# Token mixer: one lead product for v, a and b, and one logarithm and one exponential for all lengths

## The chip, the cores and the metric

The kernel runs on one core of one Trainium2 chip. The metric is the device time of one execution in microseconds (us), the median of several runs.

## What is computed

Two layers, each of a feed-forward (swiglu), a token mixer, a second feed-forward and a gated projection, each ended by a layer norm; behind them a second block with attention and a mixture of experts, which the change does not touch. There are S = 256 tokens of D = 1024. The token mixer is this (the reference, cut):

```python
proj = h @ w_in                    # sb q,k,v 3 x 256 | gdn q,k,v 3 x 512 | z 512 | a 4 | b 4 | sc 3 x 256
o_sb = stick_breaking_attention(sb_q, sb_k, sb_v)
gdn_qkv = silu(causal_dwconv(gdn_qkv, gdn_conv_w))
g_q = l2_normalize(g_q) * (GDN_HEAD_DIM ** -0.5)      # t * rsqrt(sum(t*t) + eps), over a head's 128
g_k = l2_normalize(g_k)
beta = sigmoid(gdn_b)
log_decay = -exp(gdn_a_log) * softplus(gdn_a + gdn_dt_bias)
o_gdn = gated_rms_norm(gated_delta_rule_chunked(g_q, g_k, g_v, log_decay, beta), gdn_z, gdn_norm_w)
o_sc = sc_b * causal_dwconv(sc_c * sc_h, sc_conv_w)
return concatenate([o_sb, o_gdn, o_sc]) @ w_out
```

## The kernel before, in words

Tokens lie in two halves of 128 (`t` is 0 or 1). Every large product is made three times in a reduced type, high by high, high by low and low by high part (`mm3`, L318 to L320, and the same three in `proj_T`, L559). The input of a stage is transposed on PE (`transpose_split`, L339) and split into `xTh` and `xTl`. Weights come by SP's DMAs (L254) into three raw buffers of 1 MB (`wraw`); ACT copies the high part (`whi`, L323) and DVE subtracts for the low part (`wlo`, L324), tile by tile of 512 columns. `proj` makes tokens by columns (tile `pj`); `proj_T` makes columns by tokens (tile `pT`, 256 wide, both halves at once).

Each stage's first weights are led: they are loaded and split in the tail of the stage before, four of the eight blocks of 128 rows by `start_next` (tiles `ghi`, `glo`) and the rest by `start_rest`. For the mixer these are z's 512 columns.

The mixer's order in the code (`token_mix`) is: z (`gdn_z`, led, 48 products of 512 columns); a and b (`gdn_ab`: a load of eight columns of its own, 24 products with eight output rows into `g_abT`, L588, a copy, two small transposes `g_abp`, L593, a copy); k and q of the delta rule with their convolution (`gdn_part`, L681 and L683); the gates; silu; the lengths (`gdn_norm` and `l2n`); stick-breaking's q and k; the delta rule's v; then stick-breaking's v (`usev`, 48 products of 256 columns); then the delta rule's preparation (L743 to L830) and a weave of its scan (L855 to L891) with stick-breaking's steps (tile `sb`); the short convolution (tile `sc`); the output projection.

`l2n` runs four times, for two groups of heads of k and of q: ACT squares (L692), one product with a 128 x 128 matrix of ones sums over the partitions and spreads the sum to all of them (tile `l2p`, L694, one PSUM bank at a time), ACT takes Ln and then Exp (L109, tile `l2sq`), DVE multiplies (L697). Behind each, DVE multiplies the row factors (`g_br` for k, L714; `g_eg` for q, L718). The products of k with itself (`pkk`, L755) need them.

Within an engine the order is set by a scheduler from the code's order, from priorities (`later`, `behind`) and from a model of due times; it weaves independent work between dependent steps. A matrix product in the full type (the lengths, the transposes, the delta rule's small products) and one in the reduced type alternate on PE.

Of the kernel before, what the change touches and what calls it, by code (L numbers as in the profile page):

```python
# [8 lines left out]
F32 = mybir.dt.float32  # L9
F32R = mybir.dt.float32r  # L10
I32 = mybir.dt.int32
AF = mybir.ActivationFunctionType
ALU = mybir.AluOpType
AX = mybir.AxisListType
PSUM = bass.MemoryType.PSUM
P = 128
CH = (slice(0, 64), slice(64, 128))

S = 256
D = 1024  # L20
NT = S // P
KD = D // P
# [6 lines left out]
OFF_SB = 0  # L29
OFF_GDN = 768  # L30
OFF_Z = 2304
OFF_AB = 2816
# [20 lines left out]
class Net:  # L53
# [107 lines left out]
    def masks(self):  # L161
        nc = self.nc
        g = nc.gpsimd
# [55 lines left out]
        for i in range(2):  # L219
            m = self.c([P, P], f"csel{i}")  # L220
# [5 lines left out]
        self.c_lns = self.c([P, 1], "c_lns")  # L226
        g.memset(self.c_lns, math.log(128 ** -0.5))

# [19 lines left out]
    def piece(self, src, kk, n, by=0):  # L248

        nc = self.nc  # L250
        m = kk * n
        raw = self.raw()
        rv = raw[:, :m].rearrange("p (k n) -> p k n", k=kk)
        nc.sync.dma_start(out=rv, in_=src.rearrange("(k p) n -> p k n", p=P))  # L254
        k2, n2 = (min(kk, 1024 // n), n) if by == 0 else (kk, min(n, 1024 // kk))
# [49 lines left out]
    def start_rest(self):  # L305
        if self.leads:
            src, other = self.leads.pop(0)
            if other is not None:
                self.led_p = self.piece_k(other, 2, D)
            self.led += self.piece_k(src[512:], 4, src.shape[1])  # L310
# [268 lines left out]

    def gdn_ab(self, i):  # L580

        nc, a = self.nc, self.a
        xT = self.xT
        (hi, lo), = self.piece(a["mix_w_in"][i][:, OFF_AB:OFF_AB + 8], KD, 8)
        o = self.mm_bank("g_abT")
        for k in range(KD):
            for n, (w, z) in enumerate(((hi, xT[0]), (lo, xT[0]), (hi, xT[1]))):
                nc.tensor.matmul(o[:8, :S], w[:, k], z[:, k], start=k == 0 and n == 0, stop=k == KD - 1 and n == 2)  # L588
        abT = self.s("g_abTs")
        nc.vector.tensor_copy(abT[:8, :S], o[:8, :S])  # L590
        pt = self.tr_bank("g_abp")
        for t in range(NT):
            nc.tensor.transpose(pt[:, t * 8:t * 8 + 8], abT[:8, t * P:t * P + P], self.ident[:8, :8])  # L593
        ab = self.tmp.tile([P, 8, 2], F32, name="g_ab", bufs=2)
        nc.vector.tensor_copy(ab, pt[:, :16].rearrange("p (t n) -> p n t", t=2))
        return ab

    def gdn_gates(self, i, ab):
# [88 lines left out]

    def l2n(self, src, out, bias):

        nc = self.nc  # L690
        sq = self.s("l2sq")
        nc.scalar.activation(sq, src, AF.Square)  # L692
        pn = self.tr_bank("l2p")
        nc.tensor.matmul(pn, self.ones, sq, start=True, stop=True)  # L694
        self.tact(sq, pn, AF.Ln, bias=self.c_eps)
        self.tact(sq, sq, AF.Exp, scale=-0.5, bias=bias)
        nc.vector.tensor_tensor(out, src, sq, ALU.mult)  # L697

# [9 lines left out]
    def gdn_norm(self, G, k, q):  # L708

        v = self.nc.vector  # L710
        for gr in range(2):
            eg, br = G["rows"][gr]
            self.l2n(k[gr], k[gr], 0.0)
            v.tensor_tensor(br, k[gr], br, ALU.mult)  # L714
        for gr in range(2):
            eg, br = G["rows"][gr]
            self.l2n(q[gr], q[gr], self.c_lns)
            v.tensor_tensor(eg, q[gr], eg, ALU.mult)  # L718
# [87 lines left out]

    def gdn_z(self, i):
        nc, a = self.nc, self.a
        nw = self.tmp.tile([P, P], F32, name="gdn_nw", bufs=2)
        nc.sync.dma_start(out=nw, in_=a["gdn_norm_w"][i:i + 1].broadcast_to([P, P]))  # L810
        zs = {}

        def use(t, o):
            z = zs[t] = self.s("zs")
            self.tact(z, o, AF.Silu)
            z4 = z.rearrange("p (n w) -> p n w", n=4)
            self.after(nc.vector.tensor_tensor(z4, z4, self.bc(nw, 4), ALU.mult).ins, self.ln_end)

        self.proj(a["mix_w_in"][i][:, OFF_Z:OFF_Z + 512], 512, use, lead=True)
        return zs  # L820

# [90 lines left out]

    def stick_breaking(self, i, mT):

        nc, a = self.nc, self.a
        mm = nc.tensor.matmul
        w = a["mix_w_in"][i]
        q, k, v = self.s("sbq"), self.s("sbk"), self.s("sbv")
        for dst, c0 in ((q, 0), (k, 256)):
# [4 lines left out]
        yield self.gdn_part(i, 8)  # L924

        def usev(t, o):
            nc.scalar.activation(v[:, t * 256:t * 256 + 256], o, AF.Copy)
        self.proj(w[:, 512:768], 256, usev, bank=lambda t, name: self.mm_bank(name))
        yield

# [75 lines left out]
    def token_mix(self, i):  # L1006
        a = self.a
        mT = self.new_xT()
        zs = self.gdn_z(i)
        ab = self.gdn_ab(i)  # L1010
        k, q = self.gdn_part(i, 4), self.gdn_part(i, 0)
# [7 lines left out]
        self.gdn_norm(G, k, q)  # L1019
        heads = self.stick_breaking(i, mT)  # L1020
        vc = next(heads)
# [3 lines left out]
        self.act_set(LOG_SET)  # L1025
        next(heads)
        with self.later(-1500):
# [956 lines left out]
    def run(self, stages=("f", "m", "f2", "p", "2")):  # L1984
# [4 lines left out]
        of = dict(f=lambda i: (a["ffn_w_in"][i, 0][:, :512], None),  # L1989
                  m=lambda i: (a["mix_w_in"][i][:, OFF_Z:OFF_Z + 512], None),  # L1990
                  f2=lambda i: (a["ffn_w_in"][i, 1][:, :512], None),
# [61 lines left out]
```

## Time and profile before

| | us |
|---|---|
| median of 3 runs | 1670.34 |
| lowest and highest run | 1666.17 and 1672.14 |
| profiled execution, its own time | 1672.71 |
| its span | 1670.9 |
| PE busy in the span | 1614.5 |
| DVE busy | 1289.5 |
| ACT busy | 899.0 |

The profile is of one execution. Its rows give the start or the sum and the duration in us; "x" counts instructions; `out<-in` are the program's tile names; a bracket tells how long the engine stood idle before the row and what released it. PE's records of neighbouring products overlap, so what a product occupies is the distance from one start to the next. A product in the full type leaves two records.

### The profile page before, as it was taken

To read this page: it belongs to the slowest core of one execution; us is meant where nothing else is said; L and a number is where in the kernel's file an instruction comes from. 1 tells how busy PE (TensorE), PEld (TensorE's weight loads), DVE (VectorE), ACT (ScalarE), POOL (GpSimd) and SP (SyncE) were. 2 spreads that over 40 slices of the span, in tenths; PEclk is the share of its full clock that TensorE was granted. 3 is DMA by queue.
4 is the path that set the end of the run, shared out by engine and by line. 5 is a ranking of instruction groups with operands and counts; after the bars stand their busy time and mean duration, and the time that the engine had idled before them with its cause. 6 is when DMAs were issued, how large, how long until landed. Compare 5 with 4: busy or idle time off the path is not lost.

```text
span 1670.9 us, 24511 instructions
## 1 busy us (share of the span) xinstructions
PE 1614.5 (97%) x9247; PEld 1346.8 (81%) x9247; DVE 1289.5 (77%) x2389; ACT 899.0 (54%) x1593; POOL 24.4 (1%) x90
## 2 busy tenths in 40 slices
PE   8999999999999999999999999999889889999998
PEld 6888888888888878888888888888677678787876
DVE  7669886677679786688876686697978569899896
ACT  6543374554543445543555554544575367677674
POOL 2000000000000000000000000000200000000000
PEclk9999999999999999999999999999899789999999
DMA  8667562236568656665532365685344129899995
GB/s 298 201 210 259 190 186 73 87 133 227 181 235 285 205 162 210 202 247 201 177 102 102 133 200 178 205 304 203 126 151 134 47 101 363 314 339 323 367 339 195
DMA packets 175197, 342.45 MB, mean 205 GB/s; under 512 B 12970, under 2 KB 49891, under 8 KB 175075
## 3 DMA queue, kind: packets, MB, share of 16 engines
q1 hardware_dynamic: 175074, 340.84, 59.6%
q8 instruction: 74, 1.21, 0.3%
q14 instruction: 49, 0.39, 0.1%
HBM read 339.76 MB, written 1.05 MB: 204 GB/s over the span
## 4 chain that ended last, share of the span: by engine, by line
PE 86%; DVE 7%; ACT 3%; DMA 2%; issue 1%; SPq 0%; DVEq 0%; ACTq 0%
PE gu L318 10%; PE gu L319 9%; PE gu L320 9%; PE pT L559 5%; PE y L320 5%; PE y L318 5%; PE y L319 5%; PE moe_h L319 3%; PE moe_h L320 3%; PE moe_h L318 3%; PE sc L559 2%; PE moe_y L319 2%; PE moe_y L318 2%; PE moe_y L320 2%; PE pt L339 2%; PE pj L318 2%
## 5 line engine op out<-in xcount | busy, mean ns | idle before, releaser
L324 DVE TENSOR_TENSOR wlo<-wraw,whi 128x512 fp32r<-128x512 f32 (+3 forms) x752 | 605.8, 837 | 165.2 <-ACT whi L323 162.2
L323 ACT ACTIVATE whi<-wraw 128x512 fp32r<-128x512 f32 (+3 forms) x752 | 528.4, 746 | 355.9 <-issue 98.5
L318 PE MATMUL gu<-whi,xTh 128*128 128x512 f32 (+1 forms) x736 | 274.8, 373 | 0.0
L319 PE MATMUL gu<-wlo,xTh 128*128 128x512 f32 (+1 forms) x736 | 274.2, 373 | 0.0
L320 PE MATMUL gu<-whi,xTl 128*128 128x512 f32 (+1 forms) x736 | 273.7, 372 | 0.0
L318 PEld LDWEIGHTS gu<-whi,xTh 128*128 128x128 f32 x736 | 138.7, 188 | 23.3
L320 PEld LDWEIGHTS gu<-whi,xTl 128*128 128x128 f32 x736 | 138.7, 188 | 23.2
L319 PEld LDWEIGHTS gu<-wlo,xTh 128*128 128x128 f32 x736 | 138.8, 189 | 22.7
L318 PE MATMUL y<-whi,hTh 128*128 128x512 f32 x224 | 87.7, 391 | 0.0
L320 PE MATMUL y<-whi,hTl 128*128 128x512 f32 x224 | 87.6, 391 | 0.0
L319 PE MATMUL y<-wlo,hTh 128*128 128x512 f32 x224 | 87.2, 389 | 0.0
L318 PE MATMUL y<-whi,xTh 128*128 128x512 f32 x192 | 75.9, 395 | 0.0
L320 PE MATMUL y<-whi,xTl 128*128 128x512 f32 x192 | 75.2, 392 | 0.0
L319 PE MATMUL y<-wlo,xTh 128*128 128x512 f32 x192 | 74.8, 390 | 0.0
L559 PE MATMUL pT<-xTh,whi 128*128 128x256 f32 x256 | 74.6, 291 | 0.0
L559 PE MATMUL pT<-xTh,wlo 128*128 128x256 f32 x256 | 74.4, 291 | 0.0
L559 PE MATMUL pT<-xTl,whi 128*128 128x256 f32 x256 | 73.4, 288 | 0.0
L1167 DVE SCALAR_TENSOR_TENSOR ada<-ada_w,silu_c,ada 128x512 f32<-128x512 f32 x84 | 62.7, 747 | 9.1 <-DMA ada_w<-in_w_ada_dram 8.4
L1280 DVE SCALAR_TENSOR_TENSOR bias<-rel_m,rel_delta,bias 128x384 f32<-128x384 bf16 x116 | 63.9, 613 | 0.5
L109 ACT ACTIVATE ffn_h<-gu 128x512 f32<-128x512 f32 (+1 forms) x48 | 27.0, 563 | 56.3 <-PE gu L320 56.3
L323 ACT ACTIVATE xTh<-pt 128x512 fp32r<-128x512 f32 (+1 forms) x72 | 35.6, 500 | 39.7 <-PE pt L339 34.2
L319 PE MATMUL moe_h<-wlo,moe_xh 128*128 128x512 f32 x128 | 50.8, 397 | 1.7 <-DVE wlo L324 1.7
(573 smaller groups left out, 3276.8 us busy)
## 6 DMA issues: line engine op xcount, KB each, us to landing
wraw<-in_ffn_w_in_dram SPq DMA_DIRECT2D x88, 1024.0 KB
wraw<-in_ffn_w_out_dram SPq DMA_DIRECT2D x44, 1024.0 KB
wraw<-in_mix_w_in_dram SPq DMA_DIRECT2D x28, 1024.0 KB
ada_w<-in_w_ada_dram SPq DMA_DIRECT2D x96, 256.0 KB
wraw<-in_w_gate_dram SPq DMA_DIRECT2D x20, 1024.0 KB
wraw<-in_w_up_dram SPq DMA_DIRECT2D x19, 1024.0 KB
wraw<-in_w_down_dram SPq DMA_DIRECT2D x19, 1024.0 KB
wraw<-in_mix_w_out_dram SPq DMA_DIRECT2D x8, 1024.0 KB
```

The costliest lines, as they stand in the source:

```text
L109: ins = self.nc.scalar.activation(*args, **kw).ins
L318: mm(out, l[0], r[0], start=start, stop=False)
L319: mm(out, l[0], r[1], start=False, stop=False)
L320: mm(out, l[1], r[0], start=False, stop=stop)
L323: h = self.split_hi = self.nc.scalar.activation(hi, src, AF.Copy).ins
L324: self.mark = self.nc.vector.tensor_tensor(lo, src, hi.bitcast(F32), ALU.subtract).ins
L339: self.nc.tensor.transpose(pt[:, j * P:(j + 1) * P], src[:, (c + j) * P:(c + j + 1) * P], self.ident)
L559: self.nc.tensor.matmul(o[:, :S], w[:, k], z[:, k], start=k == 0 and n == 0, stop=k == KD - 1 and n == 2)
L1167: z = nc.vector.scalar_tensor_tensor(acc, raw, c, acc, ALU.mult, ALU.add)
L1280: z = nc.vector.scalar_tensor_tensor(b, m, d, b, ALU.mult, ALU.add)
```

## The change

z and stick-breaking's v become one step at the stage's start (`mix_in`). Its second set of weights holds v's 256 columns and the eight of a and b side by side, 264 wide, and is led like z's (`led_p`, two pieces of 512 rows, four DMAs). For each half of the tokens it makes z's product and then the 264-wide one; ACT copies v, DVE copies a and b straight from PSUM. `gdn_ab` and `usev` go. `l2n` now runs once for all four: four squares, four sums with 32 columns of ones, each into its own quarter of 32 rows of one PSUM bank; one Ln and one Exp over the bank, with the bias of k on the lower 64 rows and of q on the upper 64; four products of one row each with a row of ones (tile `l2b`) spread the four results over 128 rows, and DVE multiplies from PSUM.

```diff
--- before.py
+++ after.py
@@ -224,7 +224,9 @@
         self.c_eps = self.c([P, 1], "c_eps")
         g.memset(self.c_eps, NORM_EPS)
         self.c_lns = self.c([P, 1], "c_lns")
-        g.memset(self.c_lns, math.log(128 ** -0.5))
+
+        g.memset(self.c_lns[0:64], 0.0)
+        g.memset(self.c_lns[64:P], math.log(128 ** -0.5))
 
     def bc(self, m, n):
 
@@ -251,7 +253,11 @@
         m = kk * n
         raw = self.raw()
         rv = raw[:, :m].rearrange("p (k n) -> p k n", k=kk)
-        nc.sync.dma_start(out=rv, in_=src.rearrange("(k p) n -> p k n", p=P))
+        n0 = 0
+        for z in src if isinstance(src, tuple) else (src,):
+            n1 = n0 + z.shape[1]
+            nc.sync.dma_start(out=rv[:, :, n0:n1], in_=z.rearrange("(k p) n -> p k n", p=P))
+            n0 = n1
         k2, n2 = (min(kk, 1024 // n), n) if by == 0 else (kk, min(n, 1024 // kk))
         k2 = -(-kk // -(-kk // k2))
         out = []
@@ -305,7 +311,9 @@
     def start_rest(self):
         if self.leads:
             src, other = self.leads.pop(0)
-            if other is not None:
+            if isinstance(other, tuple):
+                self.led_p = [z for k in (0, 512) for z in self.piece_k(tuple(w[k:k + 512] for w in other), 4, 264)]
+            elif other is not None:
                 self.led_p = self.piece_k(other, 2, D)
             self.led += self.piece_k(src[512:], 4, src.shape[1])
 
@@ -576,24 +584,6 @@
                 for k in range(k0, k1):
                     self.mm3(acc[t][:, :n], lhs(k, tt), pc[k - k0], k == 0, k == K - 1)
         return [use(t, acc[t][:, :n]) for t in range(NT)]
-
-    def gdn_ab(self, i):
-
-        nc, a = self.nc, self.a
-        xT = self.xT
-        (hi, lo), = self.piece(a["mix_w_in"][i][:, OFF_AB:OFF_AB + 8], KD, 8)
-        o = self.mm_bank("g_abT")
-        for k in range(KD):
-            for n, (w, z) in enumerate(((hi, xT[0]), (lo, xT[0]), (hi, xT[1]))):
-                nc.tensor.matmul(o[:8, :S], w[:, k], z[:, k], start=k == 0 and n == 0, stop=k == KD - 1 and n == 2)
-        abT = self.s("g_abTs")
-        nc.vector.tensor_copy(abT[:8, :S], o[:8, :S])
-        pt = self.tr_bank("g_abp")
-        for t in range(NT):
-            nc.tensor.transpose(pt[:, t * 8:t * 8 + 8], abT[:8, t * P:t * P + P], self.ident[:8, :8])
-        ab = self.tmp.tile([P, 8, 2], F32, name="g_ab", bufs=2)
-        nc.vector.tensor_copy(ab, pt[:, :16].rearrange("p (t n) -> p n t", t=2))
-        return ab
 
     def gdn_gates(self, i, ab):
 
@@ -685,16 +675,23 @@
 
         self.proj_T(w, use)
 
-    def l2n(self, src, out, bias):
-
-        nc = self.nc
-        sq = self.s("l2sq")
-        nc.scalar.activation(sq, src, AF.Square)
+    def l2n(self, srcs, bias):
+
+        nc = self.nc
         pn = self.tr_bank("l2p")
-        nc.tensor.matmul(pn, self.ones, sq, start=True, stop=True)
-        self.tact(sq, pn, AF.Ln, bias=self.c_eps)
-        self.tact(sq, sq, AF.Exp, scale=-0.5, bias=bias)
-        nc.vector.tensor_tensor(out, src, sq, ALU.mult)
+        rows = [slice(n * 32, n * 32 + 32) for n in range(4)]
+        for r, src in zip(rows, srcs):
+            sq = self.s("l2sq")
+            nc.scalar.activation(sq, src, AF.Square)
+            nc.tensor.matmul(pn[r], self.ones[:, :32], sq, start=True, stop=True)
+        l = self.s("l2l")
+        self.tact(l, pn, AF.Ln, bias=self.c_eps)
+        self.tact(l, l, AF.Exp, scale=-0.5, bias=bias)
+        out = [self.ch_bank("l2b") for _ in range(3)] + [self.tr_bank("l2b")]
+        for r, o in zip(rows, out):
+            r = slice(r.start, r.start + 1)
+            nc.tensor.matmul(o, self.ones[r], l[r], start=True, stop=True)
+        return out
 
     def gdn_part(self, i, c0):
 
@@ -708,13 +705,14 @@
     def gdn_norm(self, G, k, q):
 
         v = self.nc.vector
+        z = self.l2n(k + q, self.c_lns)
         for gr in range(2):
             eg, br = G["rows"][gr]
-            self.l2n(k[gr], k[gr], 0.0)
+            v.tensor_tensor(k[gr], k[gr], z[gr], ALU.mult)
             v.tensor_tensor(br, k[gr], br, ALU.mult)
         for gr in range(2):
             eg, br = G["rows"][gr]
-            self.l2n(q[gr], q[gr], self.c_lns)
+            v.tensor_tensor(q[gr], q[gr], z[2 + gr], ALU.mult)
             v.tensor_tensor(eg, q[gr], eg, ALU.mult)
 
     def gdn_prepare(self, G, k, q, vc):
@@ -804,20 +802,27 @@
             H[gr].update(X=X[gr], wT=wT, vb=vb)
         return H
 
-    def gdn_z(self, i):
+    def mix_in(self, i):
+
         nc, a = self.nc, self.a
+        xT = self.xT
         nw = self.tmp.tile([P, P], F32, name="gdn_nw", bufs=2)
         nc.sync.dma_start(out=nw, in_=a["gdn_norm_w"][i:i + 1].broadcast_to([P, P]))
-        zs = {}
-
-        def use(t, o):
+        zs, v, ab = {}, self.s("sbv"), self.tmp.tile([P, 8, 2], F32, name="g_ab", bufs=2)
+        ws = self.led, self.led_p
+        for t in range(NT):
+            tt = slice(t * P, t * P + P)
+            acc = [self.bank(t, "pj") for _ in ws]
+            for w, o in zip(ws, acc):
+                for k in range(KD):
+                    self.mm3(o[:, :w[k][0].shape[1]], (xT[0][:, k, tt], xT[1][:, k, tt]), w[k], k == 0, k == KD - 1)
             z = zs[t] = self.s("zs")
-            self.tact(z, o, AF.Silu)
+            self.tact(z, acc[0], AF.Silu)
             z4 = z.rearrange("p (n w) -> p n w", n=4)
             self.after(nc.vector.tensor_tensor(z4, z4, self.bc(nw, 4), ALU.mult).ins, self.ln_end)
-
-        self.proj(a["mix_w_in"][i][:, OFF_Z:OFF_Z + 512], 512, use, lead=True)
-        return zs
+            nc.scalar.activation(v[:, t * 256:t * 256 + 256], acc[1][:, :256], AF.Copy)
+            self.after(nc.vector.tensor_copy(ab[:, :, t], acc[1][:, 256:264]).ins, self.ln_end)
+        return zs, v, ab
 
     def gdn_values(self, H, t):
 
@@ -910,23 +915,18 @@
         tt = slice(t * P, t * P + P)
         self.transpose_split(mT[0][:, 2:6, tt], mT[1][:, 2:6, tt], y, 4)
 
-    def stick_breaking(self, i, mT):
+    def stick_breaking(self, i, v, mT):
 
         nc, a = self.nc, self.a
         mm = nc.tensor.matmul
         w = a["mix_w_in"][i]
-        q, k, v = self.s("sbq"), self.s("sbk"), self.s("sbv")
+        q, k = self.s("sbq"), self.s("sbk")
         for dst, c0 in ((q, 0), (k, 256)):
             def use(j, o, dst=dst):
                 nc.scalar.activation(dst[:, j * S:j * S + S], o, AF.Copy)
             self.proj_T(w[:, c0:c0 + 256], use)
 
         yield self.gdn_part(i, 8)
-
-        def usev(t, o):
-            nc.scalar.activation(v[:, t * 256:t * 256 + 256], o, AF.Copy)
-        self.proj(w[:, 512:768], 256, usev, bank=lambda t, name: self.mm_bank(name))
-        yield
 
         def pair(c, bank):
 
@@ -1006,8 +1006,7 @@
     def token_mix(self, i):
         a = self.a
         mT = self.new_xT()
-        zs = self.gdn_z(i)
-        ab = self.gdn_ab(i)
+        zs, v, ab = self.mix_in(i)
         k, q = self.gdn_part(i, 4), self.gdn_part(i, 0)
         self.act_set(LOG_SET)
         with self.later(-500):
@@ -1017,13 +1016,12 @@
             self.tact(z, z, AF.Silu)
         self.act_set(LOG_SET)
         self.gdn_norm(G, k, q)
-        heads = self.stick_breaking(i, mT)
+        heads = self.stick_breaking(i, v, mT)
         vc = next(heads)
         self.act_set(SILU_SET)
         for z in vc:
             self.tact(z, z, AF.Silu)
         self.act_set(LOG_SET)
-        next(heads)
         with self.later(-1500):
             H = self.gdn_prepare(G, k, q, vc)
         self.weave([self.behind(self.gdn_scan(G, H, zs, mT), -1000), heads])
@@ -1987,7 +1985,8 @@
         self.load_x()
         a = self.a
         of = dict(f=lambda i: (a["ffn_w_in"][i, 0][:, :512], None),
-                  m=lambda i: (a["mix_w_in"][i][:, OFF_Z:OFF_Z + 512], None),
+                  m=lambda i: (a["mix_w_in"][i][:, OFF_Z:OFF_Z + 512],
+                               (a["mix_w_in"][i][:, OFF_SB + 512:OFF_SB + 768], a["mix_w_in"][i][:, OFF_AB:OFF_AB + 8])),
                   f2=lambda i: (a["ffn_w_in"][i, 1][:, :512], None),
                   p=lambda i: (a["ple_w_gate"][i][:, :512], a["ple_w_proj"][i]))
         self.with_ple = "p" in stages
```

Lines move by a few numbers: L318 to L320 become L326 to L328, L323 becomes L331, L339 L347, L559 L567.

The change moves instructions, as these pieces of the orders show (engine by engine, without what other engines do between). First PE at the start of the second half of the tokens in the mixer, layer 0. Before:

```order
L320 MATMUL pj<-whi,xTl 128x512
L339 MATMUL pt<-ident,x 128x128 x8
L318 MATMUL pj<-ghi,xTh 128x512
L319 MATMUL pj<-glo,xTh 128x512
L588 MATMUL g_abT<-xTh,whi 8x256
L588 MATMUL g_abT<-xTh,wlo 8x256
```

and now:

```order
L326 MATMUL pj<-whi,xTh 128x264
L327 MATMUL pj<-wlo,xTh 128x264
L328 MATMUL pj<-whi,xTl 128x264
L347 MATMUL pt<-ident,x 128x128 x8
L326 MATMUL pj<-ghi,xTh 128x512
L327 MATMUL pj<-glo,xTh 128x512
L326 MATMUL pj<-whi,xTh 128x264
L327 MATMUL pj<-wlo,xTh 128x264
```

The transposes `pt` of the second half stood right behind z's last product of the first half; now the 264-wide products of the first half stand between. On ACT, the same place, before:

```order
L109 ACTIVATE zs<-pj 128x512
L323 ACTIVATE whi<-wraw 128x512 x3
L323 ACTIVATE xTh<-pt 128x4x128 x2
L323 ACTIVATE whi<-wraw 128x512 x5
L109 ACTIVATE zs<-pj 128x512
L323 ACTIVATE whi<-wraw 128x512 x2
```

and now:

```order
L109 ACTIVATE zs<-pj 128x512
L823 ACTIVATE sbv<-pj 128x256
L331 ACTIVATE xTh<-pt 128x4x128 x2
L331 ACTIVATE whi<-wraw 128x512 x2
L109 ACTIVATE zs<-pj 128x512
L331 ACTIVATE whi<-wraw 128x512 x5
L823 ACTIVATE sbv<-pj 128x256
```

The second half's `xTh` stood behind three `whi`; now it stands behind the copies `zs` and `sbv` of the first half. The third place is PE at the lengths, layer 0, before:

```order
L559 MATMUL pT<-xTh,whi 128x256
L559 MATMUL pT<-xTh,wlo 128x256
L694 MATMUL l2p<-l2sq,ones 128x512
L755 MATMUL pkk<-g_br,gdn_c 64x64 x16
L559 MATMUL pT<-xTl,whi 128x256
L559 MATMUL pT<-xTh,whi 128x256
L559 MATMUL pT<-xTh,wlo 128x256
```

and now:

```order
L567 MATMUL pT<-xTh,wlo 128x256
L567 MATMUL pT<-xTl,whi 128x256
L693 MATMUL l2b<-l2l,ones 128x512 x3
L753 MATMUL pkk<-g_br,gdn_c 64x64 x8
L693 MATMUL l2b<-l2l,ones 128x512
L567 MATMUL pT<-xTh,whi 128x256
L567 MATMUL pT<-xTh,wlo 128x256
L567 MATMUL pT<-xTl,whi 128x256
```

The last sum `l2p` stood in front of all 16 products `pkk`; now three spreads `l2b` stand in front of the first eight and the fourth behind them; three of the four sums stand together, 61 products ahead of the spreads. The last place is PE in the scan of the delta rule, layer 0, before:

```order
L865 MATMUL gdn_dS<-vn,kdec 128x128 x4
L320 MATMUL pj<-whi,xTl 128x256
L318 MATMUL pj<-whi,xTh 128x256
L855 MATMUL gdn_vS<-gdn_St,wT 64x128 x2
L889 MATMUL gdn_o<-gdn_St,g_eg 64x128
L891 MATMUL gdn_o<-vn,g_e 64x128
L319 MATMUL pj<-wlo,xTh 128x256
L855 MATMUL gdn_vS<-gdn_St,wT 64x128 x2
L320 MATMUL pj<-whi,xTl 128x256
```

and now:

```order
L567 MATMUL sc<-xTh,whi 128x256
L870 MATMUL gdn_dS<-vn,kdec 128x128 x4
L955 MATMUL sb<-sb_e,nsl 128x128
L956 MATMUL sb<-sb_sp,nsl 128x128
L860 MATMUL gdn_vS<-gdn_St,wT 64x128 x2
L894 MATMUL gdn_o<-gdn_St,g_eg 64x128
L896 MATMUL gdn_o<-vn,g_e 64x128
L957 MATMUL sb<-sb_e,nones 128x128
L860 MATMUL gdn_vS<-gdn_St,wT 64x128 x2
```

The products `pj` of v stood between the scan's steps; now products of the short convolution (`sc`) and stick-breaking's steps (`sb`) do.

## Rows read from the trace of the kernel before

**Rows 1.** Page, part 1: busy time, share of the span, instructions.

```profile
PE 1614.5 (97%) x9247; PEld 1346.8 (81%) x9247; DVE 1289.5 (77%) x2389; ACT 899.0 (54%) x1593; POOL 24.4 (1%) x90
```

**Rows 2.** Windows over the mixers: window, us, engines' busy us, granted clock, DMA share, GB/s.

```profile
202.90:334.80 131.90, 129.91 (x1357) 113.16 (x1357) 96.67 (x228) 72.08 (x157) 0.00 (x0) 1.00 0.39 121
794.00:926.20 132.20, 130.20 (x1349) 113.33 (x1349) 96.67 (x227) 71.64 (x155) 0.00 (x0) 0.99 0.39 121
```

**Rows 3.** Waits of PE, 180 to 360 us: total, times, longest.

```profile
PE pj L318 <- ACT xTh L323: 1.1, 1, 1.1
```

**Rows 4.** Chain that ended last, 200 to 262 us: start, us, what.

```profile
209.25 1.66 ACT whi L323 x3
210.91 0.50 ACT xTh L323
...
217.92 2.50 PE g_abT L588 x22
...
258.70 0.86 PE l2p L694 x2
```

**Rows 5.** PE's timeline, layer 1, around the transposes of a and b: start, us, what.

```profile
813.27 0.28 PE L559 MATMUL pT<-xTl,whi 128*128 128x256 f32 x1
813.39 0.28 PE L559 MATMUL pT<-xTh,whi 128*128 128x256 f32 x1
813.60 0.28 PE L593 MATMUL g_abp<-ident,g_abTs 8*128 8x8 f32 x2
...
814.04 0.28 PE L559 MATMUL pT<-xTl,whi 128*128 128x256 f32 x1
```

**Rows 6.** PE's timeline, layer 0, start of the second half.

```profile
209.03 1.29 PE L339 MATMUL pt<-ident,x 128*128 128x128 f32 x8 [0.32 <-DVE x L415]
211.45 0.50 PE L318 MATMUL pj<-ghi,xTh 128*128 128x512 f32 x1 [1.12 <-ACT xTh L323]
...
213.68 0.39 PE L318 MATMUL pj<-ghi,xTh 128*128 128x512 f32 x1
213.91 0.39 PE L319 MATMUL pj<-glo,xTh 128*128 128x512 f32 x1
```

**Rows 7.** PE's timeline, layer 0, third sum of squares and a block of small products.

```profile
255.26 0.28 PE L559 MATMUL pT<-xTh,whi 128*128 128x256 f32 x1
255.67 1.12 PE L694 MATMUL l2p<-l2sq,ones 128*128 128x512 f32 x2
...
261.75 0.28 PE L559 MATMUL pT<-xTl,whi 128*128 128x256 f32 x1
261.95 1.15 PE L743 MATMUL DT<-ident,Dm 64*64 64x64 f32 x32
263.03 0.39 PE L559 MATMUL pT<-xTh,whi 128*128 128x256 f32 x1
263.25 0.28 PE L559 MATMUL pT<-xTh,wlo 128*128 128x256 f32 x1
```

**Rows 8.** Timelines of ACT and of DVE, layer 0, at the lengths.

```profile
254.93 1.27 ACT L109 ACTIVATE l2sq<-l2p,c_eps 128x512 f32<-128x512 f32 x2
...
256.74 1.29 DVE L697 TENSOR_TENSOR gdn_c<-gdn_c,l2sq 128x512 f32<-128x512 f32 x2 [3.85 <-ACT l2sq L109]
```

**Rows 9.** Waits of SP's DMA queue, 180 to 212 us: total, times, longest.

```profile
SPq L254 <- DVE glo L324: 4.5, 1, 4.5
```

**Rows 10.** Windows of 10 us, layer 1, start of the mixer (columns as in rows 2).

```profile
795.00:805.00 10.00, 8.52 (x39) 6.45 (x38) 9.32 (x26) 4.68 (x9) 0.00 (x0) 0.89 1.01 314
```

**Rows 11.** PE's timeline, layer 1, start of the second half.

```profile
802.57 0.58 PE L318 MATMUL pj<-ghi,xTh 128*128 128x512 f32 x1 [1.13 <-ACT xTh L323]
...
806.32 0.40 PE L318 MATMUL pj<-ghi,xTh 128*128 128x512 f32 x1
```

**Rows 12.** Window at the scan's start, layer 0, tile pj alone: PE, PEld, DVE, ACT, clock, DMA.

```profile
300.00:310.00 10.00, 6.46 (x47) 5.77 (x47) 0.00 (x0) 0.38 (x1) 1.00 0.28 105
```

**Rows 13.** Window behind the scan, layer 0, tile sc alone (as in rows 12).

```profile
323.50:335.00 11.50, 6.50 (x40) 5.33 (x40) 0.00 (x0) 0.38 (x1) 1.00 0.01 1
```

## The prediction, made before the change was run

> **What bounds the kernel now.** I read the busy shares first: PE works 97% of the span, DVE 77%, ACT 54% [rows 1]. Then the change's own stretch, the token mixer, once per layer, in windows from its first z product to the last one of its output projection: PE is busy for 129.91 of 131.90 us in layer 0 and for 130.20 of 132.20 in layer 1, DVE for 96.67 and ACT for 72 [rows 2]. So only 2 us of a layer's 132 are idle on PE, and nearly everything the change can gain is PE work that it drops. DVE and ACT count only where PE waits for them, and the list of waits names one such place of size: "pj <- ACT xTh", 1.1 us, once [rows 3], where the stage's second half of tokens begins. Last I read the chain of waits for the steps that the change touches [rows 4], and PE's timeline for what each product really occupies.
>
> **The change part by part** (us per layer; PE's time unless said).
>
> *A. The product for a and b goes.* Of its 24 products 22 hold the chain for 2.50 [rows 4], 0.114 each: 24 are 2.73. The two transposes behind it stand between two pT products that start 0.65 apart (813.39, 814.04) with one more pT between; two products at their pitch of 0.12 (813.27 to 813.39) are 0.24 of that, so the transposes and the two changes of type around them cost 0.41 [rows 5]. Together -3.14. The two DVE copies go too, and two smaller ones come; DVE has room.
>
> *B. The same columns come back on v's product*, 264 wide for 256, in 48 products. A 512-column product steps by 0.23 (213.68 to 213.91 [rows 6]), a 256-column one by 0.12 [rows 5]: 0.11 for 256 columns is 0.43 ns a column, so 8 x 48 x 0.43 ns = +0.17. The 48 products themselves are only moved: 48 x 0.12 = 5.8 us from the scan to the stage's start.
>
> *C. Lengths.* Before: four sums of 512 columns at 0.86 each, the last of which stands alone in the chain [rows 4], 3.44. After: four sums that give 32 rows each, and four products of one row that spread the result over 128 rows again. Nothing in the trace has 32-row outputs. Upper bound: each as long as before, 0.86, 8 in all. Lower bound: the three sums that are issued together lie wholly over one another, 0.86, and the fourth is alone: 1.72. The nearest row is the block of 32 half-size records (64 x 64 tiles, 64 columns), 1.08 us from its start to that of the next product [rows 7], 34 ns each, where 64 columns at the sums' 0.86/2/512 would be 53 ns: neighbouring small tiles do overlap, in part. By 34/53, three sums are 1.65 and four 2.51; I take 2.75, as wide columns are not that row. The four spreads I take at 3.44: three stand together, and the k product behind them needs two DVE multiplies after the first spread (0.6 each [rows 8]), 0.86 + 1.2 + semaphores, some 2.3, which hardly lets it start before three serial spreads would be over (2.6). Sum of C: 2.75 + 3.44 - 3.44 = +2.75 (bounds +1.72 to +3.44).
>
> By the Trainium skill (TensorE: Matmul & The Clock Gate, Part 3, "Measured speedup vs the span model") three column tiles with M = 32 and N = 512 ran 2.38 times as fast as one by one; by that the three sums would be an estimated 1.08 and C +2.0. No run before the change shows that form; it is the second rival below.
>
> *D. A wait inside the lengths goes.* The third sum waits for its PSUM bank until Ln has read the first: the pT product at 255.26 occupies 0.12, the sum starts at 255.67 [rows 7], 0.29. The new sums share one bank and one Ln: -0.29.
>
> *E. Changes of type.* A block of fp32 products inside the pT products costs a little at either end: 261.75 + 0.12 to 261.95 is 0.08 before, 263.03 to 263.25 is 0.10 too long behind [rows 7]. By the order of instructions the stage has 76 such changes for 86; two of the ten are counted in A, so 8 x 0.09 = -0.72 (bounds 0, if they hide, to -0.9). D's bounds are 0, if another wait takes its place, and -0.29.
>
> *F. The start of the second half.* PE stands 0.32 before the transposes of x and 1.12 behind them, until ACT has the high half xTh [rows 6]. The chain says why: ACT makes three whi of the z weights first, 1.66, then xTh, 0.50 [rows 4]. In the new order 24 v products of the first half (24 x 0.12 = 2.9 us, plus B) stand ahead of those transposes, which covers the 0.32 and lets the layer norm of the second half end; and ACT has one zs and one sbv between instead of three whi. Left, I think: xTh's own 0.50 less the few products of old columns that go on beside it, 0.35. So -1.1 (bounds 0, when the wait only moves, to -1.44). SP now passes four more DMAs (v's 256 columns and the 8 of a and b, in two pieces of 512 rows) ahead of z's second half, which then waits for a raw buffer; SP already shows such a wait in the tail of the stage before, "glo", 4.5 us [rows 9], and PE comes to that half only after 12 z products. I cost it at nothing; the cover is that tail, and without it the transfer's lateness would show as z products that wait for whi (rival 1).
>
> *G. New waits.* One Ln and one Exp, 1.2 us of ACT back to back [rows 8], with a copy between them, now stand between the last sum and the first spread, behind 16 pT products (1.9 us): +0.15. In the scan the v products filled holes; what fills them now is the short convolution's products and stick-breaking's steps: +0.3. Together +0.45 (bounds 0 to 1.5).
>
> Sum: -3.14 + 0.17 + 2.75 - 0.29 - 0.72 - 1.1 + 0.45 = -1.88 a layer, -3.76 for two.
>
> *H. The clock.* In layer 1 the same wait is followed by products at the lower of the clock's two levels (1.2 for 2.4 GHz): the granted clock is 0.89 on the mean of these 10 us [rows 10], and from the first z product behind the wait to the seventh, with the same six others between them, it takes 3.75 us (802.57 to 806.32) where layer 0 takes 2.23 (211.45 to 213.68) [rows 6, 11]. That is 1.5 us once. A shorter wait may spare it; half is taken, -0.75.
>
> Total -4.51. The profiled execution took 1672.71 with 1670.9 of span, 2.4 above the median of the three runs, 1670.34; the sum is made on the execution and applied to the median: **1665.8** (1668.2 for a profiled execution as slow as this one). A measurement of this kernel can tell about 0.3%, 5.0 us, so the forecast lies close under that line.
>
> Ends: all bounds at the good end, -3.14 + 0.17 + 1.72 - 0.29 - 0.9 - 1.44 = -3.88 a layer, with all of H -9.3: 1661.1. All at the bad end, -3.14 + 0.17 + 3.44 + 1.5 = +1.97 a layer: 1674.3.
>
> **The rivals.**
>
> 1. *The gain is given back* (0.18). Small sums and spreads run one after another at 0.86 (C at +3.44), and the start's wait only moves from xTh to the next late thing (F at 0, H at 0): -3.14 + 0.17 + 3.44 - 0.29 - 0.72 + 0.45 = -0.09 a layer, 1670.2. For it: nothing in the trace shows sums of 32 rows overlapping. Against: the list shows only one thing late at the start, and it is ACT's order.
>
> 2. *Small tiles overlap well* (0.20). If the three sums lie almost wholly over one another (1.1 for C's lower bound of 0.86) and the spreads, which read one row each at four different places, are limited only by the two DVE multiplies (2.1 for 2.55), C is 0.8 + 0.45 lower: -1.25 a layer more, 1663.3. For it: the 34 ns of [rows 7]. Against: that row's gain is a third, not more than half. The Trainium skill's rule at C speaks for it.
>
> 3. *The scan loses its cover, slower* (0.10). In the 10 us at the scan's start 47 of v's products lie, PE is busy with them for 6.46 us [rows 12], and they fill the time in which one step of the scan waits for another; they are gone from there. If nothing takes their place, PE idles for all 5.8 us of them a layer: +11.5 - 4.5, **1677.3**. It decides from 2.3 us of such waits a layer on (the gain is then gone), and passes the 0.3% from 4.8 us. Against it: the short convolution has at least 40 products left behind the scan, 6.50 us in the 11.5 behind it [rows 13], that need only x and weights, and the new order draws them and stick-breaking's steps forward.
>
> **How the numbers follow.** The forecast has 0.52. Faster by over 0.3%: a bit under half of the forecast's own spread (0.23) and nearly all of rival 2 (0.19): 0.42. Slower by over 0.3%: rival 3, but for its mild cases: 0.09. Within: 0.49. The range from 1660.5 to 1672.5 takes in the good end, rivals 1 and 2 and most of the bad end; rival 3 is left out.
>
> **What would show it.** No product of eight rows and no 8-wide transposes; the wait of the second-half z product on xTh at 0.5 or less in both layers, and granted clock 1.00 in layer 1's first 20 us of the stage (F, H); the sums' block of three between 1.1 and 2.6 us, the spreads' block near 2.6 (C); no wait of a sum for its bank (D); the two stretches of 132 us at about 130. Wrong it would be if PE showed idle time before the state products of the scan or the first k products of over 1 us a layer (rival 3, or G mis-sized), or if the stretch stayed at 132 with the z products waiting for whi, that is for ACT or the new DMAs, instead of xTh (rival 1).

## The result and the profile after

| | before | with the change |
|---|---|---|
| median (9 runs each) | 1670.33 us | 1679.11 us |
| profiled execution, its own time | 1672.71 | 1681.59 |
| its span | 1670.9 | 1679.8 |

The ratio is 1.0066, 95% interval 1.005 to 1.0083: slower, where no change or a small gain was forecast, and outside the range. Page, part 1, of the change, for [rows 1]:

```profile
PE 1620.6 (96%) x9211; PEld 1347.5 (80%) x9211; DVE 1287.1 (77%) x2395; ACT 891.8 (53%) x1587; POOL 24.4 (1%) x91
```

PE has 36 records fewer and is busy 6.1 us longer, so the same kind of work ran more slowly somewhere. The stage shows where. (The windows of [rows 2] end with the first product of the output projection, not with the last as the prediction says; from here on the stage is taken from the first z product to the first product of the next stage.) Windows of the kernel before, layer 0, cut at z, the first sum of squares, the first pkk, the first gdn_u and the last gdn_o; columns as in [rows 2]:

```profile
203.00:249.60 46.60, 45.04 (x348) 40.83 (x349) 39.18 (x100) 28.84 (x59) 0.00 (x0) 1.00 0.64 190
249.60:259.50 9.90, 9.77 (x61) 7.37 (x60) 5.91 (x11) 8.00 (x15) 0.00 (x0) 1.00 0.55 172
259.50:298.60 39.10, 39.08 (x664) 36.31 (x663) 29.35 (x63) 15.86 (x33) 0.00 (x0) 1.00 0.23 70
298.60:323.20 24.60, 24.60 (x206) 18.81 (x205) 14.39 (x36) 12.15 (x29) 0.00 (x0) 1.00 0.29 107
323.20:374.10 50.90, 50.37 (x319) 43.75 (x318) 36.22 (x77) 29.62 (x59) 0.00 (x0) 1.00 0.32 109
```

and of the change, cut at the same places:

```profile
202.40:250.20 47.80, 47.54 (x373) 44.64 (x372) 40.45 (x103) 31.31 (x65) 0.00 (x0) 1.00 0.62 191
250.20:262.00 11.80, 10.31 (x74) 7.54 (x73) 5.24 (x11) 9.21 (x15) 0.00 (x0) 1.00 0.54 167
262.00:304.80 42.80, 42.78 (x660) 38.01 (x660) 30.25 (x64) 11.17 (x26) 0.00 (x0) 0.92 0.19 65
304.80:332.60 27.80, 25.40 (x190) 19.05 (x189) 14.70 (x36) 11.80 (x28) 0.00 (x0) 0.94 0.15 55
332.60:379.60 47.00, 46.71 (x286) 39.93 (x285) 33.48 (x72) 27.12 (x55) 0.00 (x0) 1.00 0.34 118
```

The stage grew from 171.1 to 177.2, and in layer 1 from 172.6 to 177.2: 10.7 us. The rest of the program gave 1.8 of that back. The first stretch took in v's 5.9 us and grew by only 1.2, so the start is a gain of 4.7. The stretches behind it lost more than that: PE stands still for 1.5 in the second and 2.4 in the fourth, and the granted clock is below 1 in the third and the fourth. The waits of PE, 180 to 400 us:

```profile
PE sc L567 <- DVE gdn_c L673: 2.4, 1, 2.4
PE pkk L753 <- DVE g_br L712: 1.5, 1, 1.5
PE pt L347 <- DVE x L423: 0.6, 2, 0.3
PE pj L326 <- ACT xTh L331: 0.2, 1, 0.2
```

The last row answers [rows 3]: 1.1 became 0.2, as the prediction's F says, and the start of layer 1, at a clock of 0.89 in [rows 10], is at full speed in this execution:

```profile
799.90:809.90 10.00, 9.75 (x59) 8.50 (x59) 7.68 (x24) 3.93 (x8) 0.00 (x0) 1.00 0.85 268
```

The first two waits are new. PE's timeline at the first of them, the lengths (many pT rows left out):

```profile
250.17 1.06 PE L686 MATMUL l2p<-l2sq,ones 128*32 128x512 f32 x6
251.16 0.38 PE L567 MATMUL pT<-xTh,whi 128*128 128x256 f32 x1
...
256.27 1.05 PE L686 MATMUL l2p<-l2sq,ones 128*32 128x512 f32 x2
257.24 0.38 PE L567 MATMUL pT<-xTl,whi 128*128 128x256 f32 x1
...
259.35 1.13 PE L693 MATMUL l2b<-l2l,ones 1*128 1x512 f32 x6
261.97 0.69 PE L753 MATMUL pkk<-g_br,gdn_c 128*64 128x64 f32 x16 [1.49 <-DVE g_br L712]
262.59 2.07 PE L693 MATMUL l2b<-l2l,ones 1*128 1x512 f32 x2
264.59 0.58 PE L567 MATMUL pT<-xTh,whi 128*128 128x256 f32 x1
264.97 0.41 PE L567 MATMUL pT<-xTh,wlo 128*128 128x256 f32 x1
265.18 0.41 PE L567 MATMUL pT<-xTl,whi 128*128 128x256 f32 x1
```

Three sums together take 0.99 (250.17 to 251.16), one alone 0.97; three spreads take 1.1. Then PE has nothing: DVE multiplies k, then g_br, and only then can pkk start:

```profile
260.51 0.69 DVE L711 TENSOR_TENSOR gdn_c<-gdn_c,l2b 128x512 f32<-128x512 f32 x1 [3.21 <-PE l2b L693]
261.23 0.69 DVE L712 TENSOR_TENSOR g_br<-gdn_c,g_br 128x512 f32<-128x512 f32 x1
```

Behind the wait the products are slow: the fourth spread takes 2.0, where it takes 1.05 at full speed (in e6, below), a pT 0.21 for 0.12. Windows of 10 us say that this is the clock, at the lengths and at the scan:

```profile
260.00:270.00 10.00, 8.51 (x72) 6.00 (x67) 7.44 (x15) 2.54 (x5) 0.00 (x0) 0.66 0.00 0
...
305.00:315.00 10.00, 7.60 (x65) 6.69 (x62) 5.23 (x9) 7.22 (x13) 0.00 (x0) 0.83 0.37 141
```

In the first, (1 - 0.66) x 2 x 10 = 6.8 us run at 1.2 instead of 2.4 GHz, in the second 3.4 us. If every product took twice its time there, 3.4 and 1.7 would be lost, and the expectations below reckon with that. The spread and the pT took 1.9 and 1.75 times theirs; at 1.8 times an estimated 3.0 and 1.5 are lost. PE and DVE at the scan:

```profile
306.87 0.39 PE L940 MATMUL sb<-sbq,sbk 64*128 64x128 f32 x4
309.66 0.36 PE L567 MATMUL sc<-xTh,whi 128*128 128x256 f32 x1 [2.40 <-DVE gdn_c L673]
```

```profile
306.95 1.00 DVE L673 SCALAR_TENSOR_TENSOR gdn_c<-pT,tapcols,gdn_c 128x255 f32<-128x255 f32 x2 [1.39 <-ACT gdn_c L671]
307.90 1.23 DVE L332 TENSOR_TENSOR wlo<-wraw,whi 128x1024 fp32r<-128x1024 f32 x1
309.04 0.47 DVE L673 SCALAR_TENSOR_TENSOR gdn_c<-pT,tapcols,gdn_c 128x253 f32<-128x253 f32 x1
```

PE has the short convolution's products to do, but their PSUM bank is the one from which DVE still reads the delta rule's convolution (e4 tests this), and a weight split stands between that convolution's second and third tap. In the kernel before v's products ran here.

### The profile page after: what moved, and what is told of

Its sections match the earlier page's. It is cut to its first block, busy times and chain, and to the rows that moved or that the text cites. A ratio compares the mean times of both kernels' runs of the same rounds, so it can differ in the third digit from the quotient of the medians.

```text
span 1679.8 us, 24439 instructions
## 1 busy us (share of the span) xinstructions
PE 1620.6 (96%) x9211; PEld 1347.5 (80%) x9211; DVE 1287.1 (77%) x2395; ACT 891.8 (53%) x1587; POOL 24.4 (1%) x91
## 3 DMA queue, kind: packets, MB, share of 16 engines
HBM read 339.76 MB, written 1.05 MB: 203 GB/s over the span
## 4 chain that ended last, share of the span: by engine, by line
PE 86%; DVE 9%; DMA 2%; ACT 2%; issue 1%; SPq 0%; DVEq 0%; ACTq 0%
PE gu L326 9%; PE gu L327 9%; PE gu L328 9%; PE pT L567 6%; PE y L328 5%; PE y L327 5%; PE y L326 5%; PE moe_h L327 3%; PE moe_h L328 3%; PE moe_h L326 3%; DVE wlo L332 2%; PE sc L567 2%; PE moe_y L327 2%; PE moe_y L326 2%; PE moe_y L328 2%; PE pt L347 2%
## 5 line engine op out<-in xcount | busy, mean ns | idle before, releaser
L332 DVE TENSOR_TENSOR wlo<-wraw,whi 128x512 fp32r<-128x512 f32 (+2 forms) x758 | 605.2, 829 | 160.8 <-ACT whi L331 158.4
L331 ACT ACTIVATE whi<-wraw 128x512 fp32r<-128x512 f32 (+2 forms) x758 | 528.8, 741 | 369.7 <-issue 105.4
L326 PE MATMUL gu<-whi,xTh 128*128 128x512 f32 (+1 forms) x736 | 274.8, 373 | 0.0
L328 PE MATMUL gu<-whi,xTl 128*128 128x512 f32 (+1 forms) x736 | 273.7, 372 | 0.0
L326 PEld LDWEIGHTS gu<-whi,xTh 128*128 128x128 f32 x736 | 138.7, 188 | 23.3
L328 PEld LDWEIGHTS gu<-whi,xTl 128*128 128x128 f32 x736 | 138.7, 188 | 23.3
L326 PE MATMUL y<-whi,hTh 128*128 128x512 f32 x224 | 87.7, 392 | 0.0
L328 PE MATMUL y<-whi,hTl 128*128 128x512 f32 x224 | 87.6, 391 | 0.0
L326 PE MATMUL y<-whi,xTh 128*128 128x512 f32 x192 | 75.7, 394 | 0.0
L328 PE MATMUL y<-whi,xTl 128*128 128x512 f32 x192 | 75.1, 391 | 0.0
L567 PE MATMUL pT<-xTh,whi 128*128 128x256 f32 x256 | 75.0, 293 | 0.0
L567 PE MATMUL pT<-xTh,wlo 128*128 128x256 f32 x256 | 74.6, 291 | 0.0
L567 PE MATMUL pT<-xTl,whi 128*128 128x256 f32 x256 | 74.3, 290 | 0.0
L331 ACT ACTIVATE xTh<-pt 128x512 fp32r<-128x512 f32 (+1 forms) x72 | 35.5, 500 | 40.8 <-PE pt L347 35.4
L567 PEld LDWEIGHTS pT<-xTh,whi 128*128 128x128 f32 x256 | 49.7, 194 | 5.5 <-issue 3.4
```

The lines of the kernel that those rows point to most:

```text
L326: mm(out, l[0], r[0], start=start, stop=False)
L328: mm(out, l[1], r[0], start=False, stop=stop)
L331: h = self.split_hi = self.nc.scalar.activation(hi, src, AF.Copy).ins
L332: self.mark = self.nc.vector.tensor_tensor(lo, src, hi.bitcast(F32), ALU.subtract).ins
L567: self.nc.tensor.matmul(o[:, :S], w[:, k], z[:, k], start=k == 0 and n == 0, stop=k == KD - 1 and n == 2)
```

## The experiments

The table has every run. "Stage" is the span from the first z product to the first product of the next stage in the profiled execution, layers 0 and 1; single executions differ by several us outside the mixers, so the stage tells more than the run's median. The before beside each run was measured on the same chip; the three chips of the experiments differ by up to 3 us there, so runs are compared by their ratios, which are of all runs and not of the two medians. "At half clock" is the time within each stage at which the trace shows the lower clock.

| run | median, us | before | ratio (95%) | stages, us | at half clock, us |
|---|---|---|---|---|---|
| before | 1670.33 | | | 171.1, 172.6 | 0, 3.4 |
| the change | 1679.11 | 1670.33 | 1.0066 (1.0050 to 1.0083) | 177.2, 177.2 | 10.2, 10.2 |
| e1 join only | 1671.16 | 1670.49 | 0.9998 (0.9979 to 1.0018) | 171.0, 172.7 | 0, 3.4 |
| e2 lengths only | 1683.75 | 1670.49 | 1.0085 (1.0058 to 1.0112) | 175.2, 178.3 | 3.4, 10.2 |
| e3 pkk later | 1674.08 | 1670.49 | 1.0023 (1.0007 to 1.0039) | 174.1, 174.4 | 3.4, 3.4 |
| e4 convolution's bank | 1677.30 | 1670.49 | 1.0037 (1.0022 to 1.0052) | 174.1, 174.2 | 6.8, 6.8 |
| e6 dummies at the lengths | 1674.96 | 1673.47 | 1.0020 (0.9999 to 1.0041) | 175.2, 175.2 | 3.4, 3.4 |
| e7 e3, q later | 1675.18 | 1673.47 | 1.0010 (0.9994 to 1.0027) | 176.6, 173.7 | 10.2, 3.4 |
| e8 e7 and e4 | 1669.48 | 1673.47 | 0.9965 (0.9947 to 0.9983) | 173.4, 173.3 | 6.8, 6.1 |
| e9 e1 and e4 | 1668.90 | 1673.47 | 0.9968 (0.9950 to 0.9986) | 169.5, 171.1 | 0, 3.4 |
| e10 dummies at the scan | 1679.01 | 1672.66 | 1.0032 (1.0016 to 1.0048) | 176.7, 176.8 | 6.8, 6.8 |
| e11 e8, DT later | 1663.91 | 1672.66 | 0.9943 (0.9926 to 0.9961) | 170.2, 170.2 | 0, 0 |

**e1, the join alone.** `l2n`, `gdn_norm` and `c_lns` of the kernel before, all else of the change.

> z, v, a and b as in the change, the lengths as before the change. Theory (the trace of the change shows two new waits of PE a layer, each followed by a stretch at the lower clock: pkk waits 1.49 us for g_br at the lengths, with 6.8 us at half clock, and sc waits 2.40 us for gdn_c at the scan, with 3.4 us at half clock; half of a stretch at half clock is lost): here only the scan's wait is left, 2.4 + 1.7 = 4.1 us a layer, against 3.0 us of dropped products and 1.0 of the start: even, and the dip of layer 1's start (1.5 us) is spared: 1669, within 3 us. Rival A (the led product of v, a and b and its four loads at the stage's start are what costs): as slow as the change, 1679.

Even, as the theory says and rival A does not. The scan's wait is there in both layers (2.4), the lengths' is not. Windows over the two stages:

```profile
202.20:373.30 171.10, 167.98 (x1563) 146.26 (x1563) 123.99 (x282) 93.90 (x194) 0.00 (x0) 1.00 0.38 123
792.90:965.60 172.70, 169.51 (x1563) 147.60 (x1563) 123.96 (x282) 94.20 (x194) 0.00 (x0) 0.99 0.38 121
```

Same instructions, same wait, but in layer 0 the clock stayed at full speed and in layer 1 it fell for 3.4 us: the 1.6 between them is the price of one such fall (e9's stages, 0 and 3.4 us at half clock, differ by as much), and a wait of 2.4 us does not always bring it.

**e2, the lengths alone.** The kernel before with `l2n`, `gdn_norm` and `c_lns` of the change.

> Only the lengths as in the change; z, a and b, v as before. Theory: the lengths' wait and its clock are there, 1.5 + 3.4 us a layer, the products cost 0.5 more and the bank's wait of 0.3 is gone: +5.1 a layer, +10 us: 1680, and granted clock 0.5 for some 7 us behind the spreads. Rival A (the start costs): no slower than before, 1668 to 1671.

Slower by 13 (10 were expected), with the wait of 1.5 in both layers and lower clock behind it. So the join is even, and the lengths alone cost what the whole costs, as far as the intervals tell (they overlap).

**e3, pkk behind work that is there.** `after(a, b)` orders a behind b, `sbk` holds the products pT of stick-breaking's k in order (cut):

```diff
+                z = mm(p[r, nl[n]], k[gr][:, cl[n][c]], G["rows"][gr][1][:, cl[n][c]], start=True, stop=True)
+                self.after(z.ins, self.sbk[(20, 26)[gr]])
```

> The change, but the first product pkk is ordered behind 12 products pT that follow the spreads anyhow, and the second group's pkk behind 6 more; nothing is removed. Theory: PE has work until g_br is ready, so the 1.5 us and the 3.4 us of lower clock go in both layers: -9.8, 1669.3. Rival B (the clock falls because the products of one row and of 32 rows are light, not because PE stands still): the 1.5 us go, the clock still falls: -3, 1676.

Of the 9.8, 5.0 came in the median (7.2 by the ratios) and 5.9 in the stages. pkk no longer waits and the clock stays up at the lengths though the spreads are still there, which speaks against rival B. But one step on there is a new wait:

```profile
PE sc L568 <- DVE gdn_c L674: 2.4, 1, 2.4
PE DT L742 <- DVE Dm L757: 1.4, 1, 1.4
```

DVE works k, g_br, q and g_eg off in front of Dm, so its chain is late by more than the wait that showed.

**e4, another bank for the convolution's last part.**

```diff
-        self.proj_T(w, use)
+        self.proj_T(w, use, self.tr_bank("pTv") if c0 == 10 else None)
```

> The change, but the last part of the convolution's pT has its PSUM bank in the pool of the transposes, so that the short convolution's bank does not wait for the last tap. Theory: sc's wait of 2.4 us and the 1.7 us lost at the lower clock behind it go in both layers: -8.2, 1671. Rival C (a wait costs only itself): -4.8, 1674.3. Rival D (the scan lacks work to fill, whatever bank it is in): the wait moves behind, 1679.

The stages lost 3.1 and 3.0 of the expected 4.1; the ratio went from 1.0066 to 1.0037, 4.8 us of the expected 8.2, though the medians are only 1.8 apart. The wait on gdn_c is gone, so it was the bank; smaller ones took its place:

```profile
PE pkk L753 <- DVE g_br L712: 1.5, 1, 1.5
PE sc L567 <- DVE sc_ch L991: 0.7, 2, 0.5
PE sc L567 <- ACT sc_c L987: 0.5, 1, 0.5
```

**e6, the same lateness without standing still.** The dummies (cut; pkk is ordered behind the last of them, and the comment is added here):

```diff
+                for n in range(11):      # behind the third spread, ahead of pkk
+                    d = nc.tensor.matmul(pn[:, :256], self.xT[0][:, n % 8, :P], self.xT[0][:, n % 8], start=True, stop=True)
```

> The change with 11 products of 128 x 256 in the reduced type added on PE between the three spreads and the first pkk; their result is never read, nothing else moves. They fill the 1.49 us in which PE waits for g_br, so PE is as late as before but does not stand still. Theory (standing still brings the lower clock): wait near 0, no granted clock of 0.5 behind the spreads, 3.4 us a layer less: stage 177.2 to 173.8, run 1679.1 to 1672.5. Rival B (the light products of one and 32 rows bring the lower clock): the clock still falls, 1679. If the dummies only cost (rival E, the DVE chain grows with them), slower than the change.

PE's timeline and a window of 10 us in e6:

```profile
260.40 1.13 PE L694 MATMUL l2b<-l2l,ones 1*128 1x512 f32 x6
261.46 1.58 PE L697 MATMUL l2p<-xTh 128*128 128x256 f32 x11
263.02 0.69 PE L759 MATMUL pkk<-g_br,gdn_c 128*64 128x64 f32 x16
263.64 1.12 PE L694 MATMUL l2b<-l2l,ones 1*128 1x512 f32 x2
264.69 0.39 PE L568 MATMUL pT<-xTh,whi 128*128 128x256 f32 x1
```

```profile
260.00:270.00 10.00, 9.59 (x121) 7.18 (x120) 8.41 (x17) 4.91 (x9) 0.00 (x0) 1.00 0.00 0
```

pkk starts 2.62 behind the first spread, exactly as in the change, yet the clock is 1.00 and the fourth spread takes 1.05 (263.64 to 264.69) for 2.0. Useless work made each stage 2.0 shorter and brought the ratio from 1.0066 to 1.0020. This settles the clock at this place: with the light spreads still there it falls when PE stands still behind them, and not when PE has work. It does not clear light products everywhere (last section). (3.4 were expected, an estimated 3.0 by the products' times; 0.4 went into a wait of DT for Dm that is hidden in the change, and the rest no run took apart. The scan's wait and its 3.4 us at half clock are the same in both.)

**e7, e8, e11: following the wait.** e7 adds to e3 that DVE multiplies q (`qm`) behind Dm; e8 adds e4; e11 orders the first DT behind 12 products pT too, one line of each (cut):

```diff
+            self.after(self.qm[gr], v.tensor_tensor(n2(Dm[gr]), n2(U[gr]), self.bc(self.n4, 4), ALU.mult).ins)
+        DT = mul("DT", Dm, self.ident, None, behind=self.sbk[38])
```

> As e3 (pkk behind 12 products pT), and DVE multiplies q by its spread only behind Dm, so that DT's wait for Dm, 1.37 us a layer in e3, goes. Theory (each wait moved to the next DVE step, as DVE's chain is what is late at the lengths): stage 174.1 to 172.7, run 1674.1 to 1671.3. Rival F (DVE's chain is longer than the work that PE has): the wait shows up again one step on, 1674.

> e7 with the convolution's last bank in the pool of the transposes, as in e4. Theory: e4 took 3.1 us from each stage (177.2 to 174.1), e7 takes 4.5; together 169.6 a stage, 1665, faster than before the change by some 5. Rival G (both waits hide the same lateness): one gain is lost, 1671.

> e8 with the first product DT ordered behind 12 products pT, so that its wait for Dm (1.37 us a layer in e8) is covered too. Theory: e8's stage of 173.3, of which some 3.4 went in layer 0 to the lower clock, comes to 168.5 to 169: run 1666, 2 to 3 below e8 (1669.5) and no better than e9 with the lengths of before (169.5, 1668.9). Rival F: the wait moves one step on once more, 1669.

e7 missed: DT moved up in the new order and waited for Dm as long as before (1.4), close to rival F. Its layer 0 is longer than its layer 1 because the clock fell there twice more, at the stage's start and behind DT's wait. e8 was faster than the kernel before, but missed too (169.6 was expected): its stages still show that wait, and 6 to 7 us at half clock. In e11 the wait is down to 1.0, the clock is 1.00 through both stages of the profiled execution, and its ratio is the lowest of all (a stage of 168.5 to 169 was expected):

```profile
202.50:372.70 170.20, 167.16 (x1570) 145.24 (x1571) 123.86 (x281) 90.13 (x188) 0.00 (x0) 1.00 0.38 123
792.90:963.00 170.10, 167.06 (x1569) 145.19 (x1570) 123.76 (x281) 90.14 (x188) 0.00 (x0) 1.00 0.39 123
```

At 1.6 for 3.4 us at half clock, e8's stages without their falls are an estimated 170.2 to 170.4, about e11's 170.2: what e11's stages gained on e8's is the clock.

**e9, the join and the bank, lengths as before.**

> z, v, a and b as in the change, lengths as before, the convolution's last bank as in e4. Theory: e1's stage of 171.0 less 3.1: 168, run 1665, faster than before; sums and spreads were not cheaper than the sums of before (2.0 + 2.0 against 3.4 us), so the lengths of before lose nothing against e8: within 2 us of it. Rival H (one logarithm and exponential pay on ACT or DVE elsewhere): e8 faster by 4 or more.

As fast as e8 (168 and 1665 were expected), and its undisturbed stage is the shortest of all, 169.5. Between e9 and e11 the stages favour one and the ratios the other (against before, 0.9950 to 0.9986 and 0.9926 to 0.9961); the runs don't tell them apart. What they do tell is that the new lengths, with their waits covered, are worth about nothing.

**e10, dummies at the scan.** As in e6, 36 products of 128 x 128 ahead of the short convolution's first.

> The change with 36 products of 128 x 128 in the reduced type added on PE in front of the short convolution's first product, where PE waits 2.40 us for gdn_c; their result is never read. PE is as late there as in the change, but does not stand still. Theory: no granted clock of 0.5 behind the scan's start, 1.7 us a layer less than the change where that fell in: stage 177.2 to 175.5, run 1676. The lengths' wait and its lower clock stay. Rival E (the added products cost by themselves): 1679 or more.

The clock stayed up there in both layers, but the stage lost only 0.5 of the expected 1.7. The dummies were too many: they last 4.1 for the hole of 2.4, so the first sc product does not come as late as in the change, as was expected, but 1.7 later (311.32 for 309.66); stick-breaking has a new wait (0.5) besides.

```profile
307.25 4.24 PE L952 MATMUL sb<-xTh 128*128 128x128 f32 x36
311.32 0.33 PE L568 MATMUL sc<-xTh,whi 128*128 128x256 f32 x1
```

The ratio fell from 1.0066 to 1.0032, but the intervals all but touch. Inconclusive on the price at the scan; e1 has that.

## Why the prediction was wrong, step by step

- **A, B, F right.** No product of eight rows is left; the first stretch gained 4.7 net of v's 5.9, where -3.14 + 0.17 - 1.1 = -4.1 was forecast.
- **C and D right in sum, by chance in part.** From the first sum to the first gdn_u the stage grew from 49.0 to 54.6; less some 3.0 of clock that is 2.6, where 2.75 - 0.29 + 0.15 = 2.6 stood. The sums were cheaper (2.0 for 2.75). The first spread to pkk took the forecast 2.6, but as 1.1 of work and 1.5 of standing still.
- **E miscounted.** The order of instructions has 80 changes of type in the new stage for 86, not 76; two of the six are in A, which leaves 4 x 0.09 = -0.36 for -0.72. No run shows it apart.
- **G is the step that failed.** It had 0.45 for new waits, bounded at 1.5. They were 1.49 and 2.40, 3.9 a layer. I had seen that the chain of two DVE multiplies lasts 2.3, and set it against serial spreads; with overlapping spreads (rival 2's own premise) the same chain leaves PE idle. The prediction's sign of being wrong, over 1 us idle before the first k products, is what came.
- **H had only one sign.** I let a shorter wait give the clock back and did not ask what a new wait would take: some 3.0 at the lengths and 1.6 at the scan, 4.6 us a layer, more than the waits themselves. Behind the wait for xTh the clock fell in two of four stages with the old start (1.1), and in none of 20 with the new one (0.2 to 0.3), as H hoped; but in five of these 20 it fell earlier, about the stage's first products (last section), so the new start is not always at full speed.
- **Rival 3 named the place and the side, at 0.10.** Its point of decision, 2.3 us of waiting a layer, was just reached by the scan's 2.4. Its reason was off: the work to fill the hole was there, but its PSUM bank wasn't free (e4). That its 1677.3 lies near the measured time is luck: with the scan's wait alone the run is even (e1), and the loss came with the lengths (e2).

The sum as measured, layer 0: the start +1.2 (-4.7 without v's 5.9); lengths and preparation +5.6 (1.5 of it waiting, some 3.0 clock); scan and end -0.7, where v's departure alone is -5.8 (2.4 of waiting, 1.6 of clock, and some 1.1 that no run took apart). Together +6.1, the 177.2 - 171.1 of the stage.

## What to carry to other kernels

Where PE is busy nearly all the time, an edit that makes its products cheaper has to be checked for what they hid: price each new hole as the wait plus the slow stretch that can follow it, and look on the chain of the engine behind it (here DVE) for the next late step before covering the first. When work is moved away from a place, ask which buffer the work that moves up will need there, and who still reads from it.

## What the runs showed of the hardware that was not expected

- A wait of PE of 1.5 us was followed by 3.4 to 6.8 us at half clock in both layers of all four profiles that had it at pkk; one of 2.4 at sc in nine of ten stages, one of 1.4 at DT in two of six. Filling the hole with products that nobody reads kept the clock at 1.00 and made the stage shorter (e6).
- Three sums of 32 rows, 512 columns, took 0.99 together and 0.97 alone; four spreads of one row took 1.07 to the start of the next product in one block (e3), and one alone 1.05 (e6). The Trainium skill (TensorE: Matmul & The Clock Gate, Part 3, "Measured speedup vs the span model") has 2.38 for three such column tiles; here it was 2.9. For four row tiles, of 32 rows each, it has 3.07; here, with one row each, 4 x 1.05 / 1.07 = 3.9.
- The clock also fell where PE waits for nothing: in five of the 20 stages with the new start (e4, e8, e9 and e10 in layer 1, e7 in layer 0), about the stage's first products. In front of them lie 24 products of one column each, which take 2.6 us. A sixth such fall is in e8, layer 0, behind 32 small products that take 2.7 us (wT, 290.47 to 293.14). So standing still is not the only thing that comes before a fall. Why the same products are followed by one in some stages and not in others is open; such a fall alone makes two runs' stages differ by some 1.6 us. The timeline and a window of e9, layer 1:

```profile
787.57 2.73 PE L1166 MATMUL ada_t<-ones,ada 128*128 128x1 f32 x24
...
791.71 0.63 PE L324 MATMUL pj<-ghi,xTh 128*128 128x512 f32 x1
```

```profile
790.20:800.20 10.00, 10.00 (x49) 8.51 (x50) 6.74 (x21) 2.40 (x5) 0.00 (x0) 0.83 0.80 260
```
